# Layers: attention is asked for behind a branch's first gate panel, and the key selection starts with the first value tile

## The chip, the core and the metric

The kernel runs on one core of a Trainium2 chip. The metric is the device time of one execution in microseconds (us); lower is better. The engines are named as in the profile: PE (TensorE, matmuls), DVE (VectorE), ACT (ScalarE), POOL (GpSimd), SP (SyncE, which issues the weight loads). Each engine works through its own list of instructions in the order in which the program wrote them; an instruction whose input is not ready holds up everything behind it on its engine.

## What is computed

Two blocks on 512 tokens of width 1024. The first has two layers; only the token mixing of those layers is touched here:

```
proj  = x @ w_in + b_in        # u_pool, q, k, v, iq, ik, iw, mq, gate_logits
score = sum_h relu(iq_h . ik / 8) * iw_h          # per query, over admissible keys
sel   = top 128 keys of score, per query          # n_sel = min(256, 512 // 4)
dsa   = softmax(q . k[sel] / 8) @ v[sel]          # 8 heads of 64, blocks of 128 queries
mem   = softmax(mq . mk / sqrt(128)) @ mv         # 4 heads of 128 over 256 memory rows
pool  = mean over windows 2, 4, 8, 16 minus u_pool, mixed by pool_w
merged = sum_n sigmoid(gate_n) * (branch_n @ w_br[n])   # branches 0 pool, 1 dsa, 2 mem
x = layer_norm(alpha * x + merged @ w_out);  then a mixture of experts
```

The second block (gated delta net, dilated attention, two feed-forward parts) comes after both layers and is not touched.

## The kernel before, in words

All matmuls with weights are done as three fp32r matmuls on high and low halves (`mm3`): three instructions of 512 columns per 128 rows of the contraction. Weights stream in by SP; ACT casts the high half `wH` (line 182) and DVE subtracts the low half `wL` (line 185). A Python generator per side job (`side`) is advanced by a model clock `now`: every `mm3` adds its model time (640 ns for 512 columns) and then `run_tasks` lets each job whose time has come write its next instructions. A job says by `yield` how much model time it wants to let pass. `finish(task)` writes out all that is left of a job at once. So the order of instructions on every engine is fixed when the program is built.

A layer writes, in this order:

1. The index projections (`iq`), then `mq`, then q, k and v (`qkv` panels 0, 1, 2, by `wide`, which gives the four token tiles one after another and calls `out` for each). A q or k tile goes through `rotate`: DVE adds the bias out of PSUM (`rx`, line 758), forms the rotation (`rr`, 766 to 770); PE transposes it (`tp`, 778); ACT and DVE store it (`kH`, `kL`, 782 to 786). A v tile is one DVE addition (line 723).
2. Beside them the side jobs `mem_att` (memory attention: PE `sa`, DVE maximum `mst`, ACT exponentials `mP`, PE transposes line 961) and `index` (the scores; then the selection).
3. The selection in `index` (lines 862 to 875): for each of the query blocks `qb` 1, 2, 3, with rows of W = 256, 384, 512 scores, 16 rounds of two DVE instructions, `max` (MAX8, line 869) and `match_replace` (line 870), which take out eight maxima each; then `is_equal` (872) and a POOL multiplication (873) make a mask of the score tile, and `done.add(qb)` lets the attention use it.
4. `dsa`, the attention, starts when q, k, v, the memory attention and the scores are written. Its pipeline gives one head per half gap: softmax on DVE and ACT (`P`, lines 926 to 930), PE transposes of `P` (line 890), PE `PT,v`, and the split of the result into `oTH`, `oTL`.
5. `branch(l, n, ...)` does for four panels i: a gate panel (2 x 24 matmuls, a tanh on ACT for each half, line 1035) and a product panel (2 x 12 matmuls with the branch's output, then a DVE multiplication, line 1055 or 1057). First branch 2 (mem), then `pool_branch` (two panels of 2 x 24 matmuls, DVE running sums, `mix`), then branch 0 (pool), then branch 1 (dsa, reads `oT`).

Before `pool_branch` stands `self.finish(t_idx)`: whatever is left of the selection is written there at once. `pool_branch` begins with a load of `pool_w` into a buffer (`pw`) with the tag `wk`, the same buffer in which the selection works; the load is issued by POOL, ACT casts it (`pwH`, line 979) and DVE makes the low half (`pwL`, line 980).

The second low half of k lies in a place borrowed from the weight stream (`ws.borrow`), which is given back when the attention is over.

Of the kernel before, what the change touches and what calls it, by code (L numbers as in the profile page):

```python
# [8 lines left out]
F32 = mybir.dt.float32  # L9
F32R = mybir.dt.float32r  # L10
# [7 lines left out]
S, D, NM = 512, 1024, 256  # L18
NT = S // 128
KD = D // 128  # L20
# [81 lines left out]
class XT:  # L102
# [8 lines left out]
    def need(self, ts):  # L111
        for t in sorted(t for t in self.want if t in ts):
            self.want.pop(t)()
# [119 lines left out]
class Kern:  # L233
# [422 lines left out]
    def layer(self, l, xT):  # L656
        nc, tc, A, ws = self.nc, self.tc, self.A, self.ws
        with ExitStack() as pools:
            pool = lambda n: pools.enter_context(tc.tile_pool(name=f"{n}_{l}", bufs=1, reuse_waits="tile"))
            m1 = self.m1 = pool("m1")  # L660
            iqT = m1.tile([128, 4, 512], F32, name="iqT", tag="brA")
            ikT = (m1.tile([128, 512], F32R, name="ikH"), m1.tile([128, 512], F32R, name="ikL", tag="wk"))
            iw = m1.tile([128, NT, 8], F32, name="iw")
            sct = m1.tile([128, 1280], F32, name="sc")
            sc = [sct[:, o:o + w] for o, w in ((0, 128), (128, 256), (384, 384), (768, 512))]
            rot = []
            if l:
                kv = self.mgp.tile([128, 8, 512], F32, name="mkv", tag="mg")[:, 0:4, :]
                nc.scalar.copy(kv[:, 0:2], self.kv[:, 0:2])
                nc.scalar.copy(kv[:, 2:4], self.kv[:, 2:4])  # L670
                self.kv_views(kv)
                end, X, cm = self.ln2

                def ready(t):
                    self.to_xT(X[:, t, :], t, xT)
                    next(end, None)
                for t in range(NT):
                    xT.want[t] = lambda t=t: ready(t)
            w = [ws.next(("iq", l, i)) for i in range(2)]
            bt = [self.bias(l, C_IQ + i * 256, w[i].n) for i in range(2)]  # L680
            for t in range(NT):
                for i in range(2):
                    ps = self.psum("mm", w[i].n)
                    self.tok(ps, xT, w[i], t, w[i].n)
                    rot.append(self.side(self.rotate(ps, bt[i], t, 4, iqT[:, 2 * i:2 * i + 2, :], None,
                                                     (ikT, iw) if i else None)))
                    if t == NT - 1:
                        ws.release(w[i])
            if l:
                cm.__exit__(None, None, None)  # L690
            m2 = pool("m2")
            done = set()
            t_idx = self.side(self.index(iqT, ikT, iw, sc, list(rot), done))
            mqT = m2.tile([128, 4, S], F32, name="mqT", tag="mqT")
            for i in range(2):
                w = ws.next(("mq", l, i))
                for f in range(2):
                    ps = self.psum("mm")
                    self.feat(ps, xT, w, f * 128)
                    nc.scalar.activation(mqT[:, 2 * i + f, :], ps, AF.Identity,  # L700
                                         bias=self.cols[l][:, 4 + 2 * i + f:5 + 2 * i + f])
                ws.release(w)
            brB = (m2.tile([128, 4, S], F32R, name="brH", tag="brH"),
                   m2.tile([128, 4, S], F32R, name="brL", tag="brL"))
            t_mem = self.side(self.mem_att(mqT, brB))
            kH = m2.tile([128, 4, S], F32R, name="kH")
            kL, place = None, None
            v = m2.tile([128, NT, 512], F32, name="v")
            qT = None
            for i in range(3):  # L710
                w = ws.next(("qkv", l, i))
                if i == 0:
                    qT = m2.tile([128, 4, S], F32, name="qT2", tag="qT2")
                if i == 1:
                    kL, place = ws.borrow([128, 2, S], F32R, "k")
                bt = self.bias(l, C_Q + i * 512, 512, "sig", 512)

                def out(t, ps, i=i, bt=bt):
                    if i < 2:
                        rot.append(self.side(self.rotate(ps, bt, t, 8, (qT, kH)[i], None if i else 0.125, None,  # L720
                                                         kL if i else None)))
                    else:
                        nc.vector.tensor_tensor(v[:, t], ps, bt, OP.add)
                self.wide(lambda k, t: tuple(a[:, k, t * 128:(t + 1) * 128] for a in xT), w, out)
            self.finish(t_mem, *rot)
            while "scores" not in done:
                self.step(t_idx)
            oT = (m2.tile([128, 4, S], F32R, name="oTH", tag="mqT"),
                  m1.tile([128, 4, 512], F32R, name="oTL", tag="brA"))
            t_att = self.side(self.dsa(qT, kH, kL, v, sc, oT, done))  # L730
            mg = self.mgp.tile([128, KD, S], F32, name="mg", tag="mg")
            self.branch(l, 2, xT, brB, mg, True)
            brB = (m2.tile([128, 4, S], F32R, name="brH", tag="brH"),
                   m2.tile([128, 4, S], F32R, name="brL", tag="brL"))
            self.finish(t_idx)
            t_pool = self.pool_branch(l, xT, brB)
            self.branch(l, 0, xT, brB, mg, False, need=t_pool)
            self.finish(t_att)
            ws.give_back(place)
            mT = self.branch(l, 1, xT, oT, mg, False, True)  # L740
        cm = tc.tile_pool(name=f"X{l}", bufs=1, reuse_waits="tile", side="right")
        p = cm.__enter__()
        X = p.tile([128, NT, D], F32, name="X")
        self.ln2 = self.moe_layer(l, mT, p, X), X, cm
# [88 lines left out]
    def index(self, iqT, ikT, iw, sc, before, done):  # L833

        nc, m1 = self.nc, self.m1
        nc.gpsimd.memset(sc[0], 0.0)
        nc.gpsimd.memset(sc[0][0:64, 64:128], -BIG)
        done.add(0)
        yield 6000
        self.finish(*before)  # L840
        pairs = [(qb, pr) for qb in (1, 2, 3) for pr in range(4)]
        part = lambda qb, pr: self.halves(iqT[:, pr, qb * 128:(qb + 1) * 128])
        q = part(*pairs.pop(0))
        yield 2000
        for qb in (1, 2, 3):
            W = (qb + 1) * 128
            s = sc[qb]
            for pr in range(4):
                both = self.pair(q, ikT[0][:, :W], ikT[1][:, :W])
                if pairs:  # L850
                    q = part(*pairs.pop(0))
                for h, ps in enumerate(both, 2 * pr):
                    rl = m1.tile([128, 512], F32, name="rl", tag="P", bufs=2)[:, :W]
                    nc.scalar.activation(rl, ps, AF.Relu, scale=0.125)
                    if h == 0:
                        nc.vector.tensor_scalar(s, rl, iw[:, qb, 0:1], None, op0=OP.mult)
                    else:
                        nc.vector.scalar_tensor_tensor(s, rl, iw[:, qb, h:h + 1], s, op0=OP.mult, op1=OP.add)
                yield 3000
            nc.vector.memset(s[0:64, W - 64:W], -3.0e38)  # L860
        done.add("scores")
        for qb in (1, 2, 3):
            W = (qb + 1) * 128
            s = sc[qb]
            wk = m1.tile([128, 512], F32, name="wk", tag="wk")[:, :W]
            m8 = m1.tile([128, 8], F32, name="m8")
            for r in range(16):
                src = s if r == 0 else wk
                nc.vector.max(out=m8, in_=src)
                nc.vector.match_replace(out=wk, in_to_replace=m8, in_values=src, imm_value=-3.4e38)  # L870
                yield 4 * W
            nc.vector.tensor_tensor(s, s, wk, OP.is_equal)
            nc.gpsimd.tensor_scalar(s, s, -BIG, None, op0=OP.mult)
            yield 1000
            done.add(qb)
# [145 lines left out]
            ws.release(w)  # L1021
        return t

    def branch(self, l, n, xT, br, mg, first, last=False, need=None):

        nc, m1, ws = self.nc, self.m1, self.ws
        for i in range(4):
# [17 lines left out]
                for k in (0, 2, 4):  # L1045
                    out(slice(k, k + 2))
            if need:
                self.finish(need)
            w = ws.next(("br", l, n, i))
            for f in range(2):  # L1050
                ps = self.psum("mm")
# [1352 lines left out]
```

## Time and profile before

| | us |
|---|---|
| median of 3 runs | 3045.59 (3044.25 to 3047.68) |
| the profiled execution, its own time | 3044.89 |
| its span in the profile | 3043.2 |
| PE busy | 2806.0 (92% of the span) |
| DVE busy | 1901.8 (62%) |
| ACT busy | 1284.3 (42%) |
| POOL busy | 445.7 (15%) |
| mixing of layer 0, of layer 1 | about 70 to 500, 950 to 1380 |

How to read it: PE is busy nearly all the time, so the time of the kernel is PE's work plus the holes in it and the stretches in which its clock was granted only in part. What a change of order is worth is seen in those holes, and in what ended each of them; 1.7 us of the execution lie outside the span.

### The profile page before, as it was taken

The numbers are of one execution on the slowest core, as the hardware profiler recorded it, in microseconds if no ns is written. First come the engines' busy times: TensorE is split into PE (matmuls) and PEld (weight loads), VectorE is DVE, ScalarE is ACT, GpSimd is POOL, SyncE is SP. The second block draws the span as 40 slices with busy tenths as digits, with TensorE's granted clock in tenths as the row PEclk, the third lists the DMA queues.
The fourth block names the chain that finished last, engine by engine and source line by source line (L and its number), as shares of the span: only waits on it lengthen the run. The fifth ranks groups of instructions, "written<-read, shape, count | busy, mean of one in ns | idle before, by whom it ended". The sixth has DMA issues, their size and how long they took to land. (4 is left out here: it accounts for less than half of the span.)

```text
span 3043.2 us, 38735 instructions
## 1 busy us (share of the span) xinstructions
PE 2806.0 (92%) x14315; PEld 2240.3 (74%) x14315; DVE 1901.8 (62%) x3535; ACT 1284.3 (42%) x2073; POOL 445.7 (15%) x526
## 2 busy tenths in 40 slices
PE   7989889999989898988899979999999697899998
PEld 7767668876757676777667757888888586688877
DVE  5677544798986776436799974333468636544244
ACT  3533432377863433422578832222345333322122
POOL 1000011264220000111552110000132121000000
PEclk9999999999989999999899979999999789899999
DMA  6212225899963122228799914323324400223231
GB/s 197 87 56 81 65 67 177 306 356 353 350 235 107 52 70 66 77 83 300 252 353 349 344 58 166 105 71 117 103 84 119 126 13 21 70 90 116 78 104 70
DMA packets 295587, 448.27 MB, mean 147 GB/s; under 512 B 30403, under 2 KB 155987, under 8 KB 294881
## 3 DMA queue, kind: packets, MB, share of 16 engines
q1 hardware_dynamic: 274816, 382.66, 38.3%
q0 software_dynamic: 20000, 60.99, 6.3%
q8 instruction: 114, 1.87, 0.3%
q10 hardware_dynamic: 576, 2.10, 0.2%
q14 instruction: 81, 0.66, 0.1%
HBM read 423.02 MB, written 34.65 MB: 150 GB/s over the span
## 5 line engine op out<-in xcount | busy, mean ns | idle before, releaser
L185 DVE TENSOR_TENSOR wL<-wR,wH 128x1024 fp32r<-128x1024 f32 (+2 forms) x381 | 469.2, 1254 | 269.3 <-ACT wH L182 260.2
L294 PE MATMUL mm<-xTH,wH 128*128 128x512 f32 (+1 forms) x1376 | 540.1, 393 | 0.1
L294 PE MATMUL mm<-xTH,wL 128*128 128x512 f32 (+1 forms) x1376 | 531.6, 386 | 7.5 <-DVE wL L185 7.5
L294 PE MATMUL mm<-xTL,wH 128*128 128x512 f32 (+1 forms) x1376 | 529.8, 385 | 2.3 <-DVE xTL L356 2.2
L182 ACT CAST wH<-wR 128x1024 fp32r<-128x1024 f32 (+1 forms) x394 | 399.6, 1041 | 255.1 <-PE mm L294 219.2
L294 PEld LDWEIGHTS mm<-xTH,wL 128*128 128x128 f32 x1376 | 263.2, 191 | 65.6 <-DVE wL L185 15.0
L294 PEld LDWEIGHTS mm<-xTH,wH 128*128 128x128 f32 x1376 | 264.3, 192 | 60.0 <-issue 8.9
L294 PEld LDWEIGHTS mm<-xTL,wH 128*128 128x128 f32 x1376 | 264.0, 192 | 49.8 <-DVE xTL L356 3.1
L294 PE MATMUL mm<-wH,hH 128*128 128x512 f32 (+1 forms) x608 | 241.0, 396 | 0.0
L294 PE MATMUL mm<-wH,hL 128*128 128x512 f32 (+1 forms) x608 | 239.2, 393 | 0.6 <-DVE hL L356 0.6
L294 PE MATMUL mm<-wL,hH 128*128 128x512 f32 (+1 forms) x608 | 238.6, 392 | 0.0
L294 PE MATMUL mm<-wH,xTH 128*128 128x256 f32 (+3 forms) x576 | 201.9, 351 | 10.8 <-DVE rx L758 5.3
L294 PE MATMUL mm<-wH,gH 128*96 128x512 f32 x512 | 206.7, 404 | 0.0
L294 PE MATMUL mm<-wH,gL 128*96 128x512 f32 x512 | 204.3, 399 | 0.0
L294 PE MATMUL mm<-wL,gH 128*96 128x512 f32 x512 | 203.0, 396 | 0.0
L294 PE MATMUL mm<-wH,xTL 128*128 128x256 f32 (+3 forms) x576 | 189.7, 329 | 3.6 <-DVE xTL L356 3.6
L294 PE MATMUL mm<-wL,xTH 128*128 128x256 f32 (+3 forms) x576 | 188.9, 328 | 0.0
L185 DVE TENSOR_TENSOR wL<-wX,wH 128x1024 fp32r<-128x1024 f32 x142 | 169.3, 1223 | 8.1 <-ACT wH L182 7.7
L182 ACT CAST wH<-wX 128x1024 fp32r<-128x1024 f32 x142 | 145.3, 1049 | 10.4 <-PE mm L294 9.6
L1664 DVE TENSOR_TENSOR th<-th,mm 128x512 f32<-128x512 f32 x44 | 30.3, 688 | 169.0 <-PE mm L294 169.0
L294 PEld LDWEIGHTS mm<-wH,hL 128*128 128x128 f32 (+1 forms) x608 | 107.3, 177 | 34.1 <-DVE hL L356 1.4
L294 PEld LDWEIGHTS mm<-wL,hH 128*128 128x128 f32 (+1 forms) x608 | 107.6, 177 | 30.5
(541 smaller groups left out, 5219.3 us busy)
## 6 DMA issues: line engine op xcount, KB each, us to landing
wX<-in_w SPq DMA_DIRECT2D x141, 512.0 KB, 11.3
wR<-in_w_in SPq DMA_DIRECT2D x116, 512.0 KB, 3.7
wR<-in_w SPq DMA_DIRECT2D x73, 512.0 KB, 11.0
wY<-in_w SPq DMA_DIRECT2D x69, 512.0 KB, 10.7
X<-in_w SPq DMA_DIRECT2D x56, 512.0 KB, 11.2
wZ<-in_w SPq DMA_DIRECT2D x45, 512.0 KB, 10.8
wR<-in_ffn_w_gate SPq DMA_DIRECT2D x44, 512.0 KB, 3.9
wR<-in_ffn_w_up SPq DMA_DIRECT2D x44, 512.0 KB, 4.7
```

Of the source, the lines that this page charges most:

```text
L182: nc.scalar.copy(u.H[:, :n], u.R[:, :n])
L185: eng.tensor_tensor(u.L[:, :n], u.R[:, :n], u.H[:, :n].bitcast(F32), OP.subtract)
L294: self.nc.tensor.matmul(ps, a, b, start=start, stop=stop)
L1664: nc.vector.tensor_tensor(th, th, u, OP.mult)
```

## The change

The pieces of a layer are written in another order. Three edits:

1. What branch 2 takes (the end of the memory attention and of the rotations, the scores, the start of `dsa`) is asked for by a function `attend` that `branch` calls behind its first gate panel; before, it stood ahead of the branch. For branch 1 the end of the attention and the return of the borrowed place are likewise asked for behind its first gate panel (`attended`).
2. The selection waits, before its first round, until the first v tile was written (`"turned"`).
3. A round of the selection asks for 5 W ns of model time, not 4 W.

```diff
                     else:
                         nc.vector.tensor_tensor(v[:, t], ps, bt, OP.add)
+                        done.add("turned")
                 self.wide(lambda k, t: tuple(a[:, k, t * 128:(t + 1) * 128] for a in xT), w, out)
-            self.finish(t_mem, *rot)
-            while "scores" not in done:
-                self.step(t_idx)
-            oT = (m2.tile([128, 4, S], F32R, name="oTH", tag="mqT"),
-                  m1.tile([128, 4, 512], F32R, name="oTL", tag="brA"))
-            t_att = self.side(self.dsa(qT, kH, kL, v, sc, oT, done))
-            mg = self.mgp.tile([128, KD, S], F32, name="mg", tag="mg")
-            self.branch(l, 2, xT, brB, mg, True)
+            later = {}
+
+            def attend():
+
+                if later:
+                    return
+                self.finish(t_mem, *rot)
+                while "scores" not in done:
+                    self.step(t_idx)
+                later["oT"] = (m2.tile([128, 4, S], F32R, name="oTH", tag="mqT"),
+                               m1.tile([128, 4, 512], F32R, name="oTL", tag="brA"))
+                later["att"] = self.side(self.dsa(qT, kH, kL, v, sc, later["oT"], done))
+                self.mg = self.mgp.tile([128, KD, S], F32, name="mg", tag="mg")
+
+            def attended():
+                if place in ws.places:
+                    return
+                self.finish(later["att"])
+                ws.give_back(place)
+            self.branch(l, 2, xT, brB, True, need=attend)
...
             self.finish(t_idx)
             t_pool = self.pool_branch(l, xT, brB)
-            self.branch(l, 0, xT, brB, mg, False, need=t_pool)
-            self.finish(t_att)
-            ws.give_back(place)
-            mT = self.branch(l, 1, xT, oT, mg, False, True)
+            self.branch(l, 0, xT, brB, False, need=lambda: self.finish(t_pool))
+            mT = self.branch(l, 1, xT, later["oT"], False, True, need=attended)
...
         done.add("scores")
+        while "turned" not in done:
+            yield 1000
         for qb in (1, 2, 3):
...
                 nc.vector.match_replace(out=wk, in_to_replace=m8, in_values=src, imm_value=-3.4e38)
-                yield 4 * W
+                yield 5 * W
...
             if need:
-                self.finish(need)
+                need()
+            mg = self.mg
             w = ws.next(("br", l, n, i))
```

The instructions are the same in number and kind; their order on PE, DVE and ACT differs, that on POOL and SP does not. In the changed file the lines stand 11 to 15 lower: MAX and MATCH_REPLACE are L882 and L883 (before L869 and L870), the equality L885 (L872), `pwL` L993 (L980), `kH` and `kL` L797 (L786), the softmax L939 to L943 (L926 to L930), the product of branch 2 L1070 (L1055), the transposes of `P` L903 (L890).

**Place 1.** DVE while the last k tiles are rotated, layer 0, before; `mst` belongs to the memory attention, the MAX and MATCH_REPLACE rows to the selection of query block 1:

```order
L185 TENSOR_TENSOR wL<-wR,wH 128x1024
L948 TENSOR_REDUCE mst<-sa 128x2
L949 TENSOR_SCALAR mst<-mst 128x2
L953 RECIPROCAL mst<-mst 128x2
L869 MAX m_1578<-wk 128x8
L870 MATCH_REPLACE wk<-m_1578,wk 128x256
L869 MAX m_1578<-wk 128x8
L870 MATCH_REPLACE wk<-m_1578,wk 128x256
L786 TENSOR_TENSOR kH<-tp,kH 128x2x128
L786 TENSOR_TENSOR kL<-tp,kH 128x2x128
```

The same place of the changed kernel, up to the first round of the selection:

```order
L185 TENSOR_TENSOR wL<-wR,wH 128x1024
L961 TENSOR_REDUCE mst<-sa 128x2
L962 TENSOR_SCALAR mst<-mst 128x2
L966 RECIPROCAL mst<-mst 128x2
L185 TENSOR_TENSOR wL<-wR,wH 128x1024
L723 TENSOR_TENSOR v<-mm,bt 128x512
L356 TENSOR_TENSOR brL<-sa,brH 128x512
L882 MAX m_1906<-sc 128x8
L883 MATCH_REPLACE wk<-m_1906,sc 128x256
```

No round stands ahead of the first v tile any more; before, the 16 rounds of block 1 and three of block 2 did.

**Place 2.** DVE where `pool_branch` begins, layer 0, before; `mg` is the product of branch 2's last panel, `P` the attention's softmax:

```order
L1055 SCALAR_TENSOR_TENSOR mg<-sig,mm 128x512
L872 TENSOR_TENSOR sc<-sc,wk 128x512
L356 TENSOR_TENSOR oTL<-mm,oTH 128x128
L1055 SCALAR_TENSOR_TENSOR mg<-sig,mm 128x512
L980 TENSOR_TENSOR pwL<-pw,pwH 128x512
L185 TENSOR_TENSOR wL<-wR,wH 128x1024
L356 TENSOR_TENSOR qs<-qT_1123,qs 128x128
L926 ISA P,st<-sa,sc 128x256
```

The same place of the changed kernel, from the last panel's first product to the first round behind the second one:

```order
L1070 SCALAR_TENSOR_TENSOR mg<-sig,mm 128x512
L882 MAX m_2471<-wk 128x8
L883 MATCH_REPLACE wk<-m_2471,wk 128x512
L356 TENSOR_TENSOR oTL<-mm,oTH 128x128
L1070 SCALAR_TENSOR_TENSOR mg<-sig,mm 128x512
L185 TENSOR_TENSOR wL<-wR,wH 128x1024
L882 MAX m_2471<-wk 128x8
L883 MATCH_REPLACE wk<-m_2471,wk 128x512
```

The last two of these rows stand ten times in a row, with nothing between them. Behind the tenth follows:

```order
L885 TENSOR_TENSOR sc<-sc,wk 128x512
L993 TENSOR_TENSOR pwL<-pw,pwH 128x512
L356 TENSOR_TENSOR qs<-qT_1123,qs 128x128
L939 ISA P,st<-sa,sc 128x256
L939 ISA st 128x1
L942 RECIPROCAL st<-st 128x1
L943 TENSOR_SCALAR P<-P,st 128x256
L1018 MEMSET pu 128x16
```

Ten rounds of block 3, all that `finish(t_idx)` still found to write, now stand between the end of branch 2 and the next softmax; in layer 1 it is the same. On PE the transposes of that softmax come behind the first 27 matmuls of the pool projection (before, behind 36):

```order
L294 MATMUL mm<-xTH,wH 128x512
L294 MATMUL mm<-xTL,wH 128x512
L294 MATMUL mm<-xTH,wL 128x512
L903 MATMUL tp<-ident,P 128x128 x2
L821 MATMUL sa<-kH,qs 128x256 x2
L821 MATMUL sa<-kL,qs 128x256 x2
L821 MATMUL sa<-kH,qs 128x256 x2
```

**Place 3.** PE where the attention ends, before: the last product panel of branch 0 (`br`) and the transposes of heads 29 and 30 of 32:

```order
L294 MATMUL mm<-brH,wL 128x512
L890 MATMUL tp<-ident,P 128x128 x8
L810 MATMUL sa<-kH,qs 128x512 x2
L810 MATMUL sa<-kL,qs 128x512 x2
L810 MATMUL sa<-kH,qs 128x512 x2
L294 MATMUL mm<-PT,v 64x128
```

The same in the changed kernel, where the first gate panel of branch 1 (`xT`) stands ahead:

```order
L294 MATMUL mm<-xTH,wL 128x512
L903 MATMUL tp<-ident,P 128x128 x8
L821 MATMUL sa<-kH,qs 128x512 x2
L821 MATMUL sa<-kL,qs 128x512 x2
L821 MATMUL sa<-kH,qs 128x512 x2
L294 MATMUL mm<-PT,v 64x128
```

From the eight transposes on, the rows of the attention's end are the same as before, word for word but for the line numbers, down to the last `PT,v`; behind that stood a gate panel, and now stand the products with `oT`.

## Rows read from the trace of the kernel before

**Rows 1.** Waits of PE, 60 to 500 us (layer 0): us in total, times, longest.

```profile
PE tp L890 <- DVE P L930: 14.1, 5, 5.3
PE tp L961 <- DVE kL L786: 4.4, 1, 4.4
PE mm L294 <- DVE rx L758: 2.7, 1, 2.7
...
PE sa L294 <- ACT rl L854: 1.9, 3, 0.7
PE sa L810 <- ACT mP L951: 1.7, 1, 1.7
```

**Rows 2.** Stretches: length, busy us (instructions) of PE, PEld, DVE, ACT, POOL; clock, DMA.

```profile
155.00:204.00 49.00, 40.83 (x179) 31.58 (x178) 41.36 (x107) 18.35 (x43) 0.87 (x1) 0.93 0.19 55
1026.00:1075.00 49.00, 42.34 (x180) 32.36 (x179) 41.97 (x107) 18.35 (x43) 0.88 (x1) 0.93 0.19 54
204.00:293.50 89.50, 88.07 (x413) 67.42 (x413) 71.16 (x176) 31.02 (x72) 1.17 (x1) 0.98 0.27 77
...
421.90:439.40 17.50, 9.28 (x56) 6.49 (x55) 7.33 (x16) 5.96 (x14) 1.58 (x2) 0.71 0.20 58
```

**Rows 3.** Groups of DVE instructions by line, 155 to 204 us: busy us, mean ns.

```profile
L869 DVE MAX8 m<-wk 128x8 f32<-128x256 f32 (+1 forms) x17 | 7.4, 437 | 0.2
...
L870 DVE MATCH_REPLACE8 wk<-m,wk 128x256 f32<-128x256 f32 (+1 forms) x17 | 7.2, 425 | 0.0
```

**Rows 4.** Timeline of ACT, 186 to 194 us: start, us, instruction, wait before it.

```profile
188.69 0.47 ACT L951 ACTIVATE mP<-sa,mst 128x256 f32<-128x256 f32 x1 [11.37 <-DVE mst L949]
```

**Rows 5.** Timeline of PE, 160 to 200 us, layer 0.

```profile
162.77 0.60 PE L961 MATMUL tp<-ident,mP 128*128 128x128 f32 x4
...
164.99 0.39 PE L294 MATMUL mm<-wL,xTH 128*128 128x512 f32 x1
...
192.54 1.09 PE L961 MATMUL tp<-ident,mP 128*128 128x128 f32 x4 [4.42 <-DVE kL L786]
...
196.81 0.40 PE L294 MATMUL mm<-wL,xTH 128*128 128x512 f32 x1
```

**Rows 6.** Timeline of DVE, 262 to 265 us: two rounds of block 3, back to back.

```profile
261.94 0.69 DVE L869 MAX8 m<-wk 128x8 f32<-128x512 f32 x1
...
263.45 0.70 DVE L869 MAX8 m<-wk 128x8 f32<-128x512 f32 x1
```

**Rows 7.** Timeline of DVE where the pool branch begins, 288 to 309 us.

```profile
294.42 0.69 DVE L872 TENSOR_TENSOR sc<-sc,wk 128x512 f32<-128x512 f32 x1
...
300.60 0.69 DVE L980 TENSOR_TENSOR pwL<-pw,pwH 128x512 fp32r<-128x512 f32 x1 [4.69 <-ACT pwH L979]
301.55 1.23 DVE L185 TENSOR_TENSOR wL<-wR,wH 128x1024 fp32r<-128x1024 f32 x1 [0.26 <-ACT wH L182]
...
302.89 0.42 DVE L926 CUSTOM_DVE_ANT_0 P<-sa,sc 128x256 f32<-128x256 f32 x1
```

**Rows 8.** Timeline of PE where the pool branch begins, 293 to 306 us.

```profile
294.00 0.50 PE L294 MATMUL mm<-xTH,wH 128*128 128x512 f32 x1
...
302.34 0.39 PE L294 MATMUL mm<-xTH,wL 128*128 128x512 f32 x1
304.68 0.41 PE L890 MATMUL tp<-ident,P 128*128 128x128 f32 x2 [1.96 <-DVE pu L1005]
```

**Rows 9.** Timeline of PE, start of the attention, 213 to 221 us.

```profile
215.80 0.33 PE L810 MATMUL sa<-kH,qs 64*128 64x128 f32 x2 [1.43 <-DVE qs L356]
...
220.38 0.41 PE L890 MATMUL tp<-ident,P 128*128 128x128 f32 x1
```

**Rows 10.** Timeline of PE, end of the attention, 421 to 441 us.

```profile
427.71 1.09 PE L890 MATMUL tp<-ident,P 128*128 128x128 f32 x4 [5.31 <-DVE P L930]
...
439.29 0.50 PE L294 MATMUL mm<-xTH,wH 128*128 128x512 f32 x1
```

**Rows 11.** Timeline of ACT, 160 to 225 us: the tanh of a gate half.

```profile
223.62 0.69 ACT L1035 ACTIVATE sig<-mm,cols 128x512 f32<-128x512 f32 x1 [1.00 <-issue]
```

More of the change, by code (lines that the diff above doesn't have):

```diff
@@ L1022, in pool_branch, with branch @@
         return t
-    def branch(self, l, n, xT, br, mg, first, last=False, need=None):
+    def branch(self, l, n, xT, br, first, last=False, need=None):
         nc, m1, ws = self.nc, self.m1, self.ws
```

## The prediction, made before the changed kernel ran

> **What bounds the kernel now.** PE is busy in 92% of the span, so I read its list of waits first, then the stretches around the three places that the change reorders, then the timelines of the engine that ended each wait. The list of waits of layer 0 [rows 1] holds two different things. A wait of 4.4 us for `kL` and one of 2.7 us for `rx` are rotations of k that come late; 14.1 us in five waits for `P` belong to the attention. The stretches [rows 2] place them: in 155 to 204 us, while k is rotated and until the first v tile comes, PE is busy 40.83 of 49 us, and layer 1 repeats it at 1026 to 1075 (42.34). Right behind, in 204 to 293.5 us, PE is busy 88.07 of 89.5 although DVE works 71.16. And 421.9 to 439.4, the end of the attention, has PE busy 9.28 of 17.5 us. The reader should see that DVE is full only in the first of these stretches (41.36 of 49), and that PE waits there for work that is short by itself but stands behind other work in DVE's list. Which work: 19 rounds of the selection stand in that stretch, and the 17 in its largest groups take 7.4 us for maxima and 7.2 us for replacements [rows 3]. Even ACT waits 11.37 us for a small DVE instruction of the memory attention [rows 4], and PE then waits for ACT's result through `kL` [rows 5].
>
> **Edit 2, what it takes away.** The 19 rounds leave the stretch of the k rotations (place 1). The holes there are 49 - 40.83 = 8.17 us in layer 0 and 49 - 42.34 = 6.66 in layer 1 [rows 2]. Behind the 4.42 us wait the clock is low: the same eleven instructions and the one behind them take 196.81 - 192.54 = 4.27 us, where they took 164.99 - 162.77 = 2.22 a little earlier [rows 5]; the granted clock of both layers' stretches is 0.93, so I take 2.05 for each. Relief: 8.17 + 6.66 + 4.1 = 18.9 us. It can't be more, since no hole is left there. As its lower end I take what waits remain in the stretch before, where scores and memory attention share the engines: 1.9 + 1.7 = 3.6 us per layer [rows 1], so 11.7 in all. I take 18.9, because the rotations without rounds are lighter for DVE than the scores.
>
> **Edit 2, what it adds.** The rounds are not gone; they start with the first v tile, some 49 us later on the clock of before, and there is one place by which all must be written: `finish(t_idx)` ahead of `pool_branch`. Ten rounds of block 3 are left by then and stand there in one piece (place 2). In before no round was left. What is queued behind them on DVE: the mask, `pwL`, the split of q and the softmax of the next head; and PE reaches the transposes of that head after 27 matmuls of the pool projection. Nothing else of PE's list can pass them.
>
> The working, on the clock of before. The first product of branch 2's last panel ends at 294.42, where L872 now starts [rows 7]. In the changed kernel follow there: one round, 263.45 - 261.94 = 1.51 us [rows 6]; `oTL`, about 0.3; the second product, 0.7; a `wL`, 1.23 [rows 7]: 298.1. Then ten rounds, 15.1 us: 313.2. From L872 to the softmax: `pwL` starts 300.60 - 294.42 = 6.2 us after L872 (it waits for the load of `pool_w` into the buffer that the selection just left), then `pwL` 0.69 and the split 0.28, with the `wL` at 301.55 no longer between: 7.15 us, so the softmax starts at 320.4. From its start to PE's transposes 304.68 - 302.89 = 1.79 [rows 7, 8]: 322.2. PE would be there at 304.68 - 1.96 = 302.72 after 36 matmuls; a matmul takes (302.34 - 294.00) / 36 = 0.23 us, and nine fewer stand ahead: 300.6 [rows 8]. The wait is 21.6 us where it was 1.96: 19.6 more per layer, 39 in all. Its slow stretch is already paid by the short wait of before, so I add nothing for the clock. The lower end of this term is the ten rounds alone with everything else hidden, 15.1 - (302.72 - 300.6) = 13.0 per layer; nothing in PE's list offers that cover, so I keep 19.6.
>
> [...]
>
> **Edit 3** costs nothing by itself. A job is only looked at after an `mm3` of 640 ns: 4 W is 1024, 1536 and 2048 ns, which become 1280, 1920 and 2560, and 5 W is just these. So the rounds keep the pace under which 204 to 293.5 us had no hole. In that stretch 48 - 19 = 29 rounds stood; now 48 - 10 = 38 do, 16 of them short. I estimate 4 us more DVE work per layer, against 89.5 - 71.16 = 18 us of DVE's idle time [rows 2]. I take 0; its upper end is 4 us per layer.
>
> **Edit 1, the start of the attention.** Before, PE waits 1.43 us for the split of q, and the next 12 matmuls take from 215.80 + 0.33 to 220.38, some 4.3 us, at a lowered clock [rows 9] instead of 12 x 0.23 = 2.8. The split now comes behind the gate panel; but on ACT it stands behind that panel's second tanh (0.69 us, [rows 11]), which itself waits for the panel's last matmul. The wait is moved, not removed: tanh, cast and subtraction are again more than 1 us. I take -0.5 us per layer; the ends are 0 and -3.0 (the wait and its slow stretch both gone).
>
> **Edit 1, the end of the attention.** The attention starts one gate panel later and runs at the same pace, so it is also one gate panel from its end when branch 0 is over; the panel that was to cover the end is used up by heads that before stood earlier. Place 3 shows it: from the transposes of head 29 on, the rows are those of before. The 5.31 us wait for `P` and the 17.5 us stretch [rows 2, 10] remain. Behind them the gate panel that started at 439.29 is gone, and the products need `oT`; their first nine matmuls read older heads, about 2 us, which covers the last split. I take 0.
>
> **Sum.** +39.2 - 18.9 - 1.0 = +19.3 us on the profiled execution's 3044.9, which is 0.7 below the median: 3064 us.
>
> **Rivals.**
> - *The end of the attention is covered* (not slower). If the gate panel did stand beside the last heads, PE would fill its idle 17.5 - 9.28 = 8.2 us there and run the rest at full clock; at most the whole panel, 48 x 0.23 = 11.0 us per layer. Then 39.2 - 18.9 - 1.0 - 22.0 = -2.7: 3042 us. It decides from 9.7 us per layer on. For it: it is what the moved lines ask for. Against it: the order of place 3.
> - *No relief at the rotations.* If PE's waits there came from ACT or from the memory attention's own chain and not from the rounds, the 39 us stand alone: 3083 us. Against it: ACT itself waits for DVE there [rows 4], and DVE has 8 us of slack in 49.
> - *DVE falls behind in branch 2 as well.* With the extra rounds of edit 3's paragraph not hidden, and the remaining waits of the relief's lower end: 19.3 + 8 = 3072, at worst 3079. For it: softmaxes and rounds share DVE for the whole branch. Against it: the pace is that of before.
>
> **Chances and range.** My forecast 0.72, with its own range 3056 to 3070; the covered end 0.08; no relief 0.07; DVE behind 0.13. A range of 3052 to 3078 holds the first and nearly all of the last, 0.84. It takes in the lower end of the relief (+7 us), the upper of the start (-5) and that of the extra rounds (+8). A change under 0.2%, 6 us, can't be told from none here. Faster beyond that 0.05, within it 0.06, slower 0.89.
>
> **What the profile after would show.** Right: no PE wait for `rx`, `rr` or `kL` in the rotations; one wait for `P` of 20 us or so in each layer where the pool branch starts, with ten rounds of 512 back to back on DVE just before; the same waits for `P` at the end of the attention. Wrong: if that long wait is under 10 us, or if the end of the attention shows PE busy with `xT` matmuls between its last transposes.

## The result

| | before | changed |
|---|---|---|
| median of seven executions, us | 3045.21 | 3065.91 |
| ratio, 95% interval | | 1.0082 (1.0066 to 1.0097) |
| the profiled execution, us | 3044.89 | 3059.07 |
| its span, us | 3043.2 | 3057.4 |
| PE busy, us | 2806.0 | 2795.6 |

The changed kernel is slower by 0.8%, more than the 0.2% that can be told from none. The forecast was 3064 us in 3052 to 3078. One of the seven executions of the kernel before took 4709.03 us; it is left out of the ratio and hardly moves the median.

PE's waits in layer 0 of the changed kernel, 60 to 520 us (engine, tile and line, what it waited for; us in total, times, longest), to hold against [rows 1]:

```profile
PE tp L903 <- DVE pu L1018: 21.1, 1, 21.1
PE tp L903 <- DVE P L943: 13.7, 5, 5.1
PE tp L974 <- DVE kL L797: 1.9, 1, 1.9
...
PE sa L821 <- ACT qs L355: 1.0, 1, 1.0
```

The wait for `rx` is gone, that for `kL` has fallen from 4.4 to 1.9, and one wait of 21.1 us has come; it stands under `pu`, the small DVE instruction right behind the `P` that the transposes read. Layer 1 has the same: 21.1 and 1.9. The stretches, in the columns of [rows 2], first that of the rotations, then the new wait, then as long a piece of the attention's end as was shown of before:

```profile
155.00:204.00 49.00, 47.07 (x207) 36.81 (x206) 29.87 (x61) 19.05 (x44) 0.00 (x0) 0.97 0.23 65
289.40:310.50 21.10, 0.03 (x1) 0.00 (x1) 14.19 (x33) 2.26 (x6) 2.31 (x2) 0.58 0.06 17
445.90:463.40 17.50, 9.54 (x51) 6.70 (x52) 6.75 (x16) 7.43 (x17) 0.00 (x0) 0.61 0.20 60
```

The rotations went from 40.83 us of PE work in 49 to 47.07. In the 21.1 us PE does nothing and DVE 14.19 us. At the end of the attention PE is about as idle as it was: busy 9.54 of 17.5 us, where the kernel before has 9.28.

What DVE does in that wait, in its timeline from 282 to 310 us of the changed kernel (start, us, instruction, idle time before it and what ended it):

```profile
284.81 0.68 DVE L1070 SCALAR_TENSOR_TENSOR mg<-sig,mm 128x512 f32<-128x512 f32 x1
...
286.55 0.69 DVE L882 MAX8 m<-wk 128x8 f32<-128x512 f32 x1
...
301.71 0.69 DVE L885 TENSOR_TENSOR sc<-sc,wk 128x512 f32<-128x512 f32 x1
307.93 0.69 DVE L993 TENSOR_TENSOR pwL<-pw,pwH 128x512 fp32r<-128x512 f32 x1 [5.53 <-ACT pwH L992]
...
308.74 0.42 DVE L939 CUSTOM_DVE_ANT_0 P<-sa,sc 128x256 f32<-128x256 f32 x1
```

From the first maximum at 286.55 to the mask at 301.71 lie ten rounds: 15.16 us, 1.52 each. From the mask to `pwL` it is 6.22 us, and from there 0.81 to the softmax. On PE, the last matmul before the wait and the transposes behind it:

```profile
289.05 0.39 PE L294 MATMUL mm<-xTH,wL 128*128 128x512 f32 x1
310.53 0.66 PE L903 MATMUL tp<-ident,P 128*128 128x128 f32 x2 [21.09 <-DVE pu L1018]
```

**Where the time went, by stage.** Four DVE instructions divide a layer: the first v tile, the last product of branch 2 (`mg`), the first of branch 0 (`sig`), and the first split of `mT` in the last panel of branch 1. Their rows in layer 0, first of the kernel before (its matmuls of the memory attention start at 142.60 us), then of the changed one (143.10):

```profile
204.24 0.68 DVE L723 TENSOR_TENSOR v<-mm,bt 128x512 f32<-128x512 f32 x1
295.23 0.68 DVE L1055 SCALAR_TENSOR_TENSOR mg<-sig,mm 128x512 f32<-128x512 f32 x1
358.79 1.28 DVE L1057 SCALAR_TENSOR_TENSOR sig<-sig,mm 128x512 f32<-128x512 f32 x2
501.29 3.71 DVE L356 TENSOR_TENSOR mT<-mg,mT 128x512 fp32r<-128x512 f32 x6 [8.98 <-ACT mT L355]
```

```profile
197.07 0.69 DVE L723 TENSOR_TENSOR v<-mm,bt 128x512 f32<-128x512 f32 x1 [0.87 <-PE mm L294]
...
368.63 1.28 DVE L1072 SCALAR_TENSOR_TENSOR sig<-sig,mm 128x512 f32<-128x512 f32 x2
515.94 3.71 DVE L356 TENSOR_TENSOR mT<-mg,mT 128x512 fp32r<-128x512 f32 x6 [8.98 <-ACT mT L355]
```

The `mg` row of the changed kernel is the first of the DVE timeline above. The differences of these rows, and the same in layer 1:

| stage | layer 0: before, changed, difference | layer 1: difference | both |
|---|---|---|---|
| rotations, to the first v | 61.64, 53.97, -7.67 | -8.79 | -16.5 |
| branch 2, to its last product | 90.99, 87.74, -3.25 | -3.24 | -6.5 |
| pool branch, to branch 0's first product | 63.56, 83.82, +20.26 | +18.37 | +38.6 |
| branches 0 and 1, to `mT` | 142.50, 147.31, +4.81 | +2.68 | +7.5 |
| sum | +14.15 | +9.02 | +23.2 |

The two layers are 23.2 us longer, but the profiled executions differ by 14.2 only. The other 9 us lie in the second block, which the change does not touch. Here are a stretch of the kernel before, and the piece of the changed kernel's second block where its clock was low too (columns of [rows 2]):

```profile
2480.00:2508.00 28.00, 28.00 (x152) 25.24 (x154) 8.16 (x24) 6.53 (x17) 4.20 (x6) 0.51 0.11 34
```

```profile
2517.30:2527.30 10.00, 8.69 (x48) 6.34 (x49) 5.47 (x11) 3.38 (x7) 4.16 (x3) 0.55 0.01 2
```

At `mT` of layer 1 the changed kernel is 1398.40 - 1374.98 = 23.4 us behind, at the end of the span 3057.4 - 3043.2 = 14.2. In the execution before, about half the clock (0.51) was granted for 28 us there, in the other 0.55 for about 10; I estimate from these rows some 14 us lost and some 5. Followed instruction by instruction, the lag of the changed kernel first rises to 24.5 us, falls by 2.9 shortly ahead of these two stretches, and across them from 21.4 to 14.0. The profiled execution of the changed kernel is the fastest of its seven, so the ratio of the runs is the better measure of the change; the two medians lie 20.7 us apart.

### The profile page after: what moved, and what is told of

It is laid out like the page before. It is cut to its first block, busy times and chain, and to the rows that moved or that the text cites. A ratio compares the mean times of both kernels' runs of the same rounds, so it can differ in the third digit from the quotient of the medians.

```text
span 3057.4 us, 38733 instructions
## 1 busy us (share of the span) xinstructions
PE 2795.6 (91%) x14315; PEld 2232.7 (73%) x14315; DVE 1904.3 (62%) x3535; ACT 1284.7 (42%) x2073; POOL 450.8 (15%) x526
## 5 line engine op out<-in xcount | busy, mean ns | idle before, releaser
L294 PEld LDWEIGHTS mm<-xTH,wL 128*128 128x128 f32 x1376 | 263.3, 191 | 66.0 <-DVE wL L185 15.1
```

The source lines that it names most:

```text
L294: self.nc.tensor.matmul(ps, a, b, start=start, stop=stop)
```

## The experiments

The kernels were timed against the kernel before, whose median was 3041.63 us beside e1 to e4, 3042.38 beside e5 to e8 and 3043.34 beside e9 and e10. None of them leaves out a part of the computation. In the edits and in the rows `...` stands for lines that are not shown.

**e1, edits 1 and 3 alone.**

```diff
-        while "turned" not in done:
-            yield 1000
```

> The changed kernel without the wait for the first v tile (edits 1 and 3 alone). My theory: the 21 us waits of PE at the pool branch come from the rounds that are left over, so they go (under 3 us each), the waits at the k rotations come back (about 4.4 and 2.7 us in layer 0), and the time is that of the kernel before, about 3044 us (ratio 1.000, within 0.003). Rival: the attention that starts a gate panel later makes the softmax late, whatever the rounds do; then a wait over 15 us stays in each layer and the time is 3060 or more.

Measured: 3038.94 us, ratio 0.9988 (0.9978 to 0.9997). PE's waits in layer 0 at the pool branch (`pu`) and at the rotations, the same in layer 1:

```profile
PE tp L972 <- DVE kL L797: 4.4, 1, 4.4
PE mm L294 <- DVE rx L769: 2.7, 1, 2.7
PE tp L901 <- DVE pu L1016: 2.1, 1, 2.1
```

The theory holds and the rival falls: the later attention does not make the softmax late. These two edits alone gain at most a little: some 3.6 us by the ratio, 1 to 7 by its interval, which is hardly more than the 0.2% that can't be told from none. The four marks in layer 0:

```profile
205.69 0.68 DVE L723 TENSOR_TENSOR v<-mm,bt 128x512 f32<-128x512 f32 x1
...
292.48 0.68 DVE L1068 SCALAR_TENSOR_TENSOR mg<-sig,mm 128x512 f32<-128x512 f32 x1
355.66 1.28 DVE L1070 SCALAR_TENSOR_TENSOR sig<-sig,mm 128x512 f32<-128x512 f32 x2
501.53 3.70 DVE L356 TENSOR_TENSOR mT<-mg,mT 128x512 fp32r<-128x512 f32 x6 [8.98 <-ACT mT L355]
```

Branch 2 takes 86.79 us here, 4.2 less than before, and the stage from `sig` to `mT` 145.87, 3.4 more; in layer 1 it is 4.2 less and 2.8 more. So edit 1 shortens branch 2 and lengthens the end by most of that: the attention's matmuls stand a panel later.

**e2, edit 2 alone**, put into the kernel before.

```diff
                         nc.vector.tensor_tensor(v[:, t], ps, bt, OP.add)
+                        done.add("turned")
...
         done.add("scores")
+        while "turned" not in done:
+            yield 1000
```

> The kernel before with the wait for the first v tile alone (edit 2). My theory: all of the loss comes from it: one wait of PE of about 21 us in each layer where the pool branch starts, no waits for rx or rr at the k rotations, 3062 to 3070 us (ratio 1.006 to 1.008). Rival (the later attention is the cause): no such wait, 3045 us or less.

Measured: 3064.74 us, ratio 1.0073 (1.0058 to 1.0087), one long wait in each layer (21.1 us in layer 1), none for `rx`:

```profile
PE tp L893 <- DVE pu L1008: 21.2, 1, 21.2
```

Edit 2 is the loss. Its marks in layer 0:

```profile
198.40 0.69 DVE L723 TENSOR_TENSOR v<-mm,bt 128x512 f32<-128x512 f32 x1 [0.88 <-PE mm L294]
...
291.19 0.68 DVE L1058 SCALAR_TENSOR_TENSOR mg<-sig,mm 128x512 f32<-128x512 f32 x1
373.16 1.28 DVE L1060 SCALAR_TENSOR_TENSOR sig<-sig,mm 128x512 f32<-128x512 f32 x2
515.72 3.71 DVE L356 TENSOR_TENSOR mT<-mg,mT 128x512 fp32r<-128x512 f32 x6 [8.98 <-ACT mT L355]
```

The end, `sig` to `mT`, takes 142.56 us, as before (142.50). In layer 1 the end is 0.6 us shorter than before. So the 7.5 us that the changed kernel loses there belong to edit 1, which alone shows 6.1 of them (e1). That edit 1 gains 3.6 us alone and shows no gain on top of edit 2 (1.0082 and 1.0073) is within the intervals.

**e5, edit 3 undone.**

```diff
-                yield 5 * W
+                yield 4 * W
```

> The changed kernel with 4 W in place of 5 W (edit 3 undone). The instruction lists of all five engines are word for word those of the changed kernel, so my theory that edit 3 does nothing by itself has no rival but a number that enters elsewhere: waits of 21.1 us at the pool branch as in the changed kernel, 3060 to 3068 us (ratio 1.005 to 1.009). It also says how far two measurements of one program lie apart.

Measured: 3065.77 us, ratio 1.0091 (1.0065 to 1.0117), wait 21.2 us. By its instruction lists it is the same program, so edit 3 does nothing, and two measurements of one program came out 0.0009 apart.

**e3, fewer rounds left over:** the selection let go at the last k tile.

```diff
                         rot.append(self.side(self.rotate(ps, bt, t, 8, (qT, kH)[i], None if i else 0.125, None,
                                                          kL if i else None)))
+                        if i and t == NT - 1:
+                            done.add("turned")
...
                         nc.vector.tensor_tensor(v[:, t], ps, bt, OP.add)
-                        done.add("turned")
```

> The changed kernel with the selection let go at the last k tile, not at the first v tile: five rounds of block 3 are left over where ten were, and three rounds stand again between the last rotations. My theory: a wait at the pool branch is the left-over rounds times 1.51 us plus what stays, so 21.1 - 5 x 1.51 = 13.5 us in each layer; with at most 3 us per layer of the waits at the rotations back, 3048 to 3058 us (ratio 1.001 to 1.004). Rival (the load of pool_w and the mask behind it set the wait, the rounds are hidden beside them): 18 us or more, 3063 or more.

Measured: 3048.61 us, ratio 1.0026 (1.0015 to 1.0037). Its waits of PE in layer 0 at the two places:

```profile
PE tp L904 <- DVE pu L1019: 13.5, 1, 13.5
PE tp L975 <- DVE kL L798: 2.2, 1, 2.2
```

Five rounds fewer, 7.6 us less waiting, 1.52 a round: nothing hides them. And the wait at the rotations hardly moved (2.2 for 1.9).

**e6, the load ahead of the rounds.** The wait holds, beside ten rounds, 5.5 us in which DVE stands still for `pwH`. POOL's timeline in the changed kernel, 300 to 312 us, shows what the load of `pool_w` stands behind:

```profile
302.48 1.49 POOL L886 TENSOR_SCALAR sc<-sc 128x512 f32<-128x512 f32 x1 [35.00 <-DVE sc L885]
304.04 0.82 POOL L991 DMA_DIRECT2D pw<-in_pool_w  x1
```

The multiplication of the last mask is ahead of it in POOL's list, so by the order of this list a buffer of its own would not be enough, and the issue has to move too. This run moves both at once, so it does not show the buffer alone. The tile `ikH` gets a tag of its name, in a line not shown. In these two rows the issue starts at 304.04 us, right behind the multiplication's end at 302.48 + 1.49 = 303.97.

```diff
-        pw = m1.tile([128, 4, 128], F32, name="pw", tag="wk")
+        pw = m1.tile([128, 4, 128], F32, name="pw", tag="ikH")
...
         nc.gpsimd.dma_start(pw, self.A["pool_w"][l].rearrange("g c e -> c g e"))
+        self.finish(t_idx)
         nc.scalar.copy(pwH, pw)
...
-            self.finish(t_idx)
-            t_pool = self.pool_branch(l, xT, brB)
+            t_pool = self.pool_branch(l, xT, brB, t_idx)
```

> The changed kernel with pool_w in the buffer that ikH leaves, and its load issued ahead of the last rounds, not behind the last mask. Only POOL's order changes. My theory: the long wait is ten rounds and a load in a row, so the 5.5 us that DVE stands still for pwH go: the wait at the pool branch is 21.1 - 5.5 = 15.6 us in each layer, 3052 to 3058 us (ratio 1.002 to 1.005). Rival: POOL's multiplication of the mask (1.49 us) or the transposes' own chain holds PE as well; then the wait stays above 19 us and the time near 3064.

Measured: 3051.62 us, ratio 1.0028 (1.0018 to 1.0038). The wait is the same in both layers:

```profile
PE tp L902 <- DVE pu L1018: 15.9, 1, 15.9
```

DVE's timeline there, 295 to 312 us:

```profile
302.04 0.69 DVE L884 TENSOR_TENSOR sc<-sc,wk 128x512 f32<-128x512 f32 x1
302.65 0.68 DVE L993 TENSOR_TENSOR pwL<-pw,pwH 128x512 fp32r<-128x512 f32 x1
```

`pwL` follows the mask at once, and PE still waits for all that stands ahead. The wait is a sum along DVE's list, as the prediction built it.

**e4, the rounds spread out.** `pw` and `pd` move to the buffer of `ikH`, whose last reader is the scores (`ikH` gets the same tag as in e6), and the selection runs on beside the pool branch. Like e6, this also takes the load of `pool_w` out from behind the mask.

```diff
-        pw = m1.tile([128, 4, 128], F32, name="pw", tag="wk")
+        pw = m1.tile([128, 4, 128], F32, name="pw", tag="ikH")
...
-                d = m1.tile([128, S], F32, name="pd", tag="wk")
+                d = m1.tile([128, S], F32, name="pd", tag="ikH")
...
-            self.finish(t_idx)
             t_pool = self.pool_branch(l, xT, brB)
+            self.finish(t_idx)
```

> The changed kernel in which pool_w and the differences of the pool branch take the buffer that ikH leaves, so that the selection keeps its own and may run on: its last ten rounds stand one by one between the instructions of the pool branch. The number of rounds is the same. My theory: the long wait goes (under 4 us), the relief at the rotations stays, 3022 to 3035 us (ratio 0.992 to 0.997). Rival: DVE's work is the price wherever it stands, so the 15 us of rounds come back as waits of PE inside the pool branch and the time is that of the kernel before or worse, 3042 to 3060.

Measured: 3027.86 us, ratio 0.9955 (0.9941 to 0.9969). The waits of PE in layer 0:

```profile
PE tp L903 <- DVE P L943: 11.7, 4, 5.1
PE sa L294 <- ACT pdH L355: 5.4, 1, 5.4
PE sa L821 <- DVE pu L1018: 2.8, 1, 2.8
```

The 21.1 us are gone, at the price of a 5.4 us wait for `pdH` that I had not expected. In DVE's timeline the first of the ten rounds and the mask behind the tenth are

```profile
286.04 0.69 DVE L882 MAX8 m<-wk 128x8 f32<-128x512 f32 x1
...
332.66 0.69 DVE L885 TENSOR_TENSOR sc<-sc,wk 128x512 f32<-128x512 f32 x1
```

so they lie over 46.6 us and no longer in 15.2. Of the 21.1 us the load was 5.2 (e6); the other 15.9 go when the same ten rounds, as long as before, stand between other work. It was not DVE's load, but the order.

**e7, both ideas together.** The edits are those of e3 and e4.

> The last two ideas together: the selection is let go at the last k tile, and runs on into the pool branch, where now five rounds stand in place of ten. My theory: rounds in the pool branch are what made PE wait 5.4 us for pdH when the selection ran on from the first v tile; with five of them ending two groups earlier that wait goes, and the waits at the rotations stay at 2.2 us: 3014 to 3025 us (ratio 0.991 to 0.995). Rival: the pdH wait belongs to the pool branch's own chain (running sums, cast, split) and stays; then 3028 or more.

Measured: 3025.04 us, ratio 0.9937 (0.9924 to 0.9950); the wait for `pdH` is gone, that for `P` is 15.2 us in five. The theory of the wait holds; the time is at the slow edge of its range (3025), and it overlaps with that of e4, so a gain over e4 is not shown.

**e8, the attention started ahead again**, on top of e7.

```diff
-            self.branch(l, 2, xT, brB, True, need=attend)
+            attend()
+            self.branch(l, 2, xT, brB, True)
```

> The same, with the attention started ahead of branch 2 as in the kernel before, and its end still asked for behind the first gate panel of branch 1 (the first half of edit 1 undone). My theory of the end: the gate panel covered nothing because the attention began a panel later; here only one group of eight transposes stands uncovered, in place of waits of 5.1, 0.5 and 2.3 us. Gain 3 to 6 us per layer against the run without it, less up to 1.5 us at the start of the attention: 3006 to 3022 us (ratio 0.988 to 0.994). Rival: the last softmax is late by itself and the start costs what the end gives: no difference to the run without it.

Measured: 3020.58 us, ratio 0.9929 (0.9916 to 0.9942). At the attention's end PE's timeline, 415 to 470 us, has one wait where there were three (5.1, 0.5 and 2.3):

```profile
437.22 1.09 PE L905 MATMUL tp<-ident,P 128*128 128x128 f32 x4 [4.86 <-DVE P L945]
```

At its start PE waits 2.3 us instead of 1.0. The mechanism is there; the gain in time over e7 cannot be told from none, as the intervals overlap.

**e9 and e10, faster heads**, on top of e7 and of e8.

```diff
-        yield from self.pipeline(items, stages, 4300, lambda qb, h: qb in done)
+        yield from self.pipeline(items, stages, 3800, lambda qb, h: qb in done)
```

> The kernel of e7 (edit 1 kept, selection let go at the last k tile and running on) with a head gap of 3800 in place of 4300 model ns: half a gap is then three matmul steps and not four, so the attention runs a quarter faster and its last head ends within the first gate panel of branch 1. My theory: the uncovered end (waits of 5.1, 0.5 and 2.3 us and a slow stretch behind them) was set by when the attention ends, not by the softmax; it goes, 8 to 12 us per layer: 3001 to 3010 us (ratio 0.986 to 0.990). Rival: nine matmuls (some 2.1 us) no longer cover the 2.0 us chain of a softmax; then most of the 32 heads wait a few tenths to one us each, the gain is eaten and the time is 3020 to 3040.

> The kernel of e8 (the attention also started ahead of branch 2) with the same head gap of 3800. My theory: once the end is covered in both, the earlier start is worth nothing more and costs the wait of 2.3 us and the slow stretch where the attention starts: the time of e9 or up to 5 us above it. Rival: the earlier start leaves more matmuls beside each softmax, so it is faster than e9 by 3 us or more.

Measured: 3003.52 us, ratio 0.9879 (0.9859 to 0.9900), for the first; 3022.00, ratio 0.9940 (0.9925 to 0.9955), for the second. The first is the fastest kernel of this study, 40 us under the kernel before by the medians (30 to 43 by the interval). Its profile is that of the longest of its five executions, 3025.55 us, with a mean granted clock of 0.953 where the other four have 0.961 to 0.964. Ahead of the second block its gain is there in full: `mT` of layer 1 starts at 1337.56 us, where it was 1374.98; of these 37.4 us, 3043.2 - 3023.9 = 19.3 are left at the end of the span. Its waits of PE for `P` in layer 0:

```profile
PE tp L904 <- DVE P L944: 8.0, 5, 5.8
```

The waits at the attention's end are gone. The last transposes of `P` in its timeline, 395 to 460 us, follow the matmul ahead of them without a wait:

```profile
405.14 0.60 PE L904 MATMUL tp<-ident,P 128*128 128x128 f32 x4
```

Some softmaxes are now uncovered elsewhere, the longest for 5.8 us in the pool branch. The rival said so of most heads; it came for five, and they cost less than the end did. In the second kernel the waits for `P` in layer 0 are

```profile
PE tp L905 <- DVE P L945: 11.8, 6, 3.6
```

and the time is 18 us above the first. Both of my expectations missed this: neither "up to 5 us above" nor "faster" is what came. By the four marks it takes, in layer 0, 7.3 us more in branch 2 and 4.1 more in the pool stage, and 3.7 less at the end; its `mT` of layer 1 starts at 1352.36 us, 14.8 behind the first kernel. So most of the 18 us arises in the two mixings. All its waits of PE in layer 1 together come to some 5 us more than in the first; why the rest is lost I did not settle.

## Why the prediction was right

The time, the sign and the mechanism held; of its signs, one did not come: a wait for `kL` stayed in the rotations, 1.9 us. By its steps:

- **Edit 2, what it adds**: forecast +39.2 us for both layers, measured +38.6 in the stage. The wait was forecast at 21.6 us and is 21.1. Its parts held one by one: ten rounds 15.1 (15.16), mask to `pwL` 6.2 (6.22), softmax to transposes 1.79 (308.74 to 310.53, 1.79). That the rounds count in full is shown by e3 (five fewer take 7.6 us off), and that the load of `pool_w` counts by e6 (5.2 us off). The pitch of a round is 1.52 us, and its rows add up to nearly that: the maximum takes 0.69, the load of the eight values 0.09 and the replacement 0.68 (changed kernel, the round at 286.55 us).
- **Edit 2, what it takes away**: forecast -18.9, measured -16.5. This term was mis-sized. I took it that no hole would stay in the rotations, because they are lighter for DVE than the scores; 1.93 us stay in each layer, 3.9 in all. The shortfall is only 2.4, because PE's own work in this stage became 5.5 us shorter in both layers together (the granted clock of layer 0's stage was 0.94 before and 0.97 in the changed kernel), where I had allowed 4.1 for the clock; so two errors in part cancel. ACT's timeline of the changed kernel, 182 to 186 us, shows what the last k tile stands behind:

```profile
182.35 0.47 ACT L964 ACTIVATE mP<-sa,mst 128x256 f32<-128x256 f32 x1 [4.71 <-DVE mst L962]
...
183.60 0.91 ACT L968 ACTIVATE mP<-mP,mst 128x256 f32<-128x256 f32 x2 [0.23 <-DVE mst L966]
184.41 1.05 ACT L793 CAST kH<-tp 128x512 fp32r<-128x512 f32 x2
```

  The cast of `kH` comes behind the exponentials and scalings of the memory attention. So part of the rival "no relief" was true: of the wait for `kL` (4.42 us in layer 0) about half came from ACT and the memory attention's own chain. That this is the cause is read from the order of these rows; no run changed it. It fits that e3, with three rounds back between the rotations, has 2.2 us there for 1.9.
- **Edit 1, the start**: forecast -1.0. Beside the wait (0.96 for 1.43) the slow stretch went too. PE's timeline of the changed kernel, from the wait to the first transposes of `P`:

```profile
218.81 0.65 PE L821 MATMUL sa<-kH,qs 64*128 64x128 f32 x6 [0.96 <-ACT qs L355]
219.39 0.50 PE L294 MATMUL mm<-brH,wH 128*128 128x512 f32 x1
...
222.31 0.27 PE L903 MATMUL tp<-ident,P 128*128 128x128 f32 x1
```

  The twelve matmuls from 219.39 to 222.31 take 2.9 us at a granted clock of 1.00, where they took 4.3 [rows 9] at 0.63. With the wait that is 1.8 us a layer, inside the ends that I gave (0 to -3.0) but not what I chose (-0.5). The stage gained 6.5 us in all, 3.2 a layer: by e1 edit 1 took 4.2 a layer off it, more than half of which is work moved to the end, and by e2 edit 2 put 1.8 on, of which 0.9 is a longer wait for `qs` that edit 1 takes away again.
- **Edit 1, the end**: forecast 0, measured +7.5 in the stage. The order argument held: the three waits are 5.06, 0.54 and 2.25 us where they were 5.31 [rows 10], 0.55 and 2.25, and the panel in front of them covers nothing. The first of them in the changed kernel:

```profile
450.95 1.09 PE L903 MATMUL tp<-ident,P 128*128 128x128 f32 x4 [5.06 <-DVE P L943]
```

  What I left out is that heads which no longer stand in branch 2 must stand later. e1 and e2 show it: +3.4 and +2.8 us with edit 1 alone, 0.1 and -0.6 with edit 2 alone. The two stages together are +1.0 for the -1.0 forecast, so the slip cost little. That they nearly cancel was in no step of the prediction: here the sum was lucky.
- **Edit 3**: 0, as forecast; the lists are the same.

The sum by stages is 23.2 us against the forecast 19.3. The runs say 0.8%, 25 us, with an interval of 20 to 30, so the forecast lies just under it, and the medians say 20.7. Of the rivals, the covered end did not happen (it takes faster heads, e9), and of DVE behind in branch 2 there is at most a little: with edit 2 alone branch 2 took 92.79 us for 90.99, of which 0.9 is a longer wait for `qs` at the start of the attention.

## What to carry to other kernels

When work is postponed, look for the place by which it must be written out. If it arrives there in one piece, what stands behind it in that engine's list waits for the sum, however much idle time the engine has in the stage before: here PE waited 21.1 us, although DVE had been busy only 73.56 of the 87.74 us of branch 2. Spread between other instructions the same ten rounds cost PE little (e4: the 21.1 us wait went, waits of 5.4 and 2.8 came). A buffer that two jobs share can be the only reason for such a place, and a buffer whose last reader is long past removes it. And a side job that starts later also ends later by the same amount of work, so a panel put in front of its end covers nothing unless the job also runs faster (e9); started early again, the same panel covered two of three waits (e8).

## What the hardware showed that I had not expected

- PE was granted about half its clock while it was fully busy: 28.00 of 28 us busy at 0.51, in the second block of the kernel before. In the 50 us ahead of that stretch PE was busy 48.91 us at 1.00. The changed kernel, with the same second block, has about 10 us at 0.55. The profile of e3 has PE busy 174.25 of 200 us at 0.73 from 2400 to 2600 us, where the kernel before has 162.81 at 0.84. The profiled executions of e3 and e9 are the longest of their runs, 27 and 22 us above the medians, with a mean granted clock of 0.942 and 0.953, where the others have 0.948 to 0.953 and 0.961 to 0.964. So single executions of one program differ: e3 ran from 3045.08 to 3076.02 us.
- After the 21 us wait the lower clock cost little more than after the 1.96 us wait of before: in the 5.3 us behind the wait (310.53 to 315.80 us) 0.50 was granted, where it was 0.68 (304.68 to 310.00), and the pool stage grew by 18.4 to 20.3 us for 19.1 us more of waiting.
